# Where the transposes of the small convolution rows stand: among the keys' projections or in the dilated attention

## The chip, the core and the metric

One core of a Trainium2 chip runs the whole kernel in one launch. The metric is device time in microseconds of one execution; a kernel's time is the median over several executions. The engines spoken of here are TensorE (PE, with its weight loads, PEld), VectorE (DVE), ScalarE (ACT), GpSimd (POOL) and SyncE (SP), whose queue issues all DMA transfers of this kernel.

## The reference, cut to what matters

The kernel computes one layer of a decoder trunk on 256 positions and 1024 channels, in float32. A token mixer has three branches that read one input projection: block-sparse attention (8 heads), a short gated convolution, and dilated attention (12 heads in 3 groups). A gated feed-forward part with its own depthwise convolution follows, and each half ends in a residual and a layer norm.

```python
y_conv = b_gate * causal_dwconv(c_gate * hc, w_short_conv)      # 3 taps x 512 channels
y_dil = dilated_mixture(heads(qd, DIL_HEADS), heads(kd, DIL_HEADS), heads(vd, DIL_HEADS))
...
u = causal_dwconv(x @ w_up, w_ffn_conv) + b_ffn_conv            # 3 taps and a bias x 5632 channels
gate, val = jnp.split(u, 2, axis=-1)
return (jax.nn.silu(gate) * val) @ w_down
```

The change concerns the small operands `w_short_conv`, `w_ffn_conv` and `b_ffn_conv`. They lie in memory as rows along the channels; the convolutions want one number per channel, with the channels on the partitions.

## The kernel before, in words

**Matrix products.** Every float32 product is made of three matmuls (`mm3`, lines 229 to 231) on operands that are split into a high and a low part. A split is a cast on ACT (line 168) and a subtraction on DVE (line 169). The weights come through three `raw` buffers of 1 MB; each is split into four pieces of 128x512, up to ten pieces ahead of their use (`prep`, `LEAD`).

**The order of the work.** `project` makes two halves of 24 matmuls of 256 columns each into an `acc` buffer (three of them), and `by_tokens` makes steps of 12 matmuls of 512 columns. After each half or step stands a `tick`. It prepares the next weight pieces, consumes the result if one is complete, and takes one function off the list `side`. So `side` spreads the attention's work between the projections. A planner then puts the instructions of each engine in an order of its own: an instruction written later may be moved ahead into a place where the engine would stand idle by the planner's reckoning. The buffers of one pool are handed out in the order in which the code first writes them; in the program of before this holds for all 70 `att` buffers and all 759 `b` buffers without an exception.

**Around the change.** The stage runs: the dilated attention's queries (the third group by line 523), its keys (three groups, six halves and six ticks, lines 526 and 527), its values (`project_tokens` with four ticks, `project_tokens_half` with two), then the values of the block-sparse attention (`project_tokens` again, four ticks, line 534), then the short convolution's C and h (lines 552 and 553). `keys` consumes a half on ACT (lines 311 and 313) and DVE (lines 317 and 318); the last line-318 subtraction frees the `acc` buffer. `dilated` gives seven functions for each of two head pairs `p` and `q`: scores, second scores, normalisation, two turns by transposes (line 347), the product with the values, and the outputs. Scores are matmuls of line 326 into `att` buffers, of which there are five.

**The small rows.** `small_loads` issues five DMAs on SP's queue into `row1` and `row2`, which take 2 of the 61 `b` buffers. `small_weights` transposes them: one transpose of 12 rows (line 484) and four of 44 rows (line 486) on PE into one `att` buffer, then two copies on DVE, to `sconv` (line 487) and to `fconv` (line 488). `sconv` is first read by line 547 in the short convolution, `fconv` by `taps` (lines 700 and 702) in the feed-forward part.

Of the kernel before, what the change touches and what calls it, by code (L numbers as in the profile page):

```python
# [37 lines left out]
def trunk(ctx: ExitStack, tc, x, w_in, w_short_conv, w_moba_proj, w_dil_proj, w_conv_proj, w_mix_out,  # L38
# [133 lines left out]
    side, late = [], []  # L172
# [90 lines left out]
    def project_tokens():  # L263

        vs = [(buf(F32R, (P, 2, 256)), buf(F32R, (P, 2, 256))) for _ in range(2)]

        def consume(t, o):
            for i, (vh, vl) in enumerate(vs):
                split(o[:, 256 * i:256 * i + 256], vh[:, t, :], vl[:, t, :])

        by_tokens(of_x, KT, consume)
        return vs
# [16 lines left out]
    def queries(store):  # L289

        def consume(c, o):
            q = buf(F32R, (P, 2, T))
            for a in range(2):
                s = HALF[a]
                nc.scalar.copy(q[s, a, :], o[s, :])
            for a in range(2):
                s, n = HALF[a], HALF[1 - a]
                nc.vector.tensor_sub(q[n, a, :], o[s, :], q.bitcast(F32)[s, a, :])  # L298
            store.append(q)
        return consume  # L300
# [116 lines left out]
    def moba(c, q, k, v, y):  # L417
        es, en, ps = [], [], []

        def score():  # L420
            e1, e0 = etiles()
            es.extend((e1, e0))
            for a in range(2):
                o = att((P, 2, T))
                for t in range(2):
                    scores(o[:, t, :], q[c], k[c], a, t)
                e = e1[:, a * T:a * T + T], e0[:, a * P:a * P + P]
                en.append(exponentials(e[0], [(e[0], o[:, 1, :], maskm.rearrange("p a c -> p (a c)"))]))
                en.append(exponentials(e[1], [(e[1], o[:, 0, 0:P], maskm[:, 1, :])]))

        def normal():
            while en:
                normalized(*en.pop(0))

        def turn():
            e1, e0 = es
            p0 = turned([e0[:, 0:P], e1[:, 0:P], e0[:, P:2 * P], e1[:, 2 * P:3 * P]])
            h, l = turned([e1[:, P:2 * P], e1[:, 3 * P:4 * P]])
            ps.append((p0, (h[:, 0:2, :], l[:, 0:2, :])))

        def value():
            ps.append(values([v], ps, c))

        return [score, normal, turn, value, lambda: outputs(ps[1], y)]

    def both(*fs):
        return lambda: [f() for f in fs]
# [27 lines left out]
    def small_loads():  # L475
        nc.sync.dma_start(row1[0:12], w_short_conv.rearrange("j (t c) -> (j t) c", c=P))
        for j in range(3):
            nc.sync.dma_start(row2[0:2 * NJ, j, :], w_ffn_conv[j].rearrange("(t c) -> t c", c=P))
        nc.sync.dma_start(row2[0:2 * NJ, 3, :], b_ffn_conv[0].rearrange("(t c) -> t c", c=P))
# [37 lines left out]
    for g in range(2):  # L517
        q = queries(dq[g])
# [3 lines left out]
    for g in range(2, 3):  # L522
        project(queries(dq[g]), ahead=0)
    small_loads()
    side += [lambda: None] * 4 + [small_weights]
    for g in range(3):
        project(keys(dk[g]), ahead=0)
    assert not side
    yd = [buf(F32R, (P, 2, T)) for _ in range(2)]
    p, q = (dilated(c, dq, dk, dv, [t[:, c, :] for t in yd]) for c in range(2))  # L530
    side += [p[0], p[1], p[2], q[0], p[3], p[4], q[1], p[5], q[2], p[6], q[3], q[4], q[5], q[6]]
    dv.extend(project_tokens())
    dv.append(project_tokens_half())
    mv = project_tokens()
# [3 lines left out]
    for b in range(2):  # L538
# [21 lines left out]
        p, q = (moba(c, mq, mk, mv[b], [t[:, c, :] for t in ym]) for c in range(2))  # L560
# [244 lines left out]
```

## Time and profile before

| what | value |
|---|---|
| median of 3 runs | 476.15 us (474.7, 476.15, 476.85) |
| profiled execution | 475.9 us, of which the span from the first to the last instruction is 474.1 us |
| busy share of PE, DVE, ACT | 98%, 75%, 57% of the span |
| data moved | 83.45 MB, mean 176 GB/s |
| mean granted TensorE clock | 0.992 of full speed |

The profile is one execution. Times in its views are microseconds from the start of the span. A row of the timeline gives the start, the duration, the engine, the line, the operation, the tile written and the tiles read, and, in brackets, how long the engine stood idle before and what ended that. Matmuls are pipelined: each lasts longer than the distance from its start to the next one's, so costs on PE are read as distances between starts.

### The profile page before, as it was taken

The numbers are of one execution on the slowest core, as the hardware profiler recorded it, in microseconds if no ns is written. First come the engines' busy times: TensorE is split into PE (matmuls) and PEld (weight loads), VectorE is DVE, ScalarE is ACT, GpSimd is POOL, SyncE is SP. The second block draws the span as 40 slices with busy tenths as digits, with TensorE's granted clock in tenths as the row PEclk, the third lists the DMA queues.
The fourth block names the chain that finished last, engine by engine and source line by source line (L and its number), as shares of the span: only waits on it lengthen the run. The fifth ranks groups of instructions, "written<-read, shape, count | busy, mean of one in ns | idle before, by whom it ended". The sixth has DMA issues, their size and how long they took to land.

```text
span 474.1 us, 8155 instructions
## 1 busy us (share of the span) xinstructions
PE 463.7 (98%) x3095; PEld 426.3 (90%) x3095; DVE 355.5 (75%) x756; ACT 268.4 (57%) x568; POOL 10.4 (2%) x29
## 2 busy tenths in 40 slices
PE   8989999999999999999999999999999999999993
PEld 6989898999999888888888899999999999999983
DVE  5895998678989944775477966997767686786866
ACT  4894585736667844634463325876565565664710
POOL 1100000010100000000000000000000000000000
PEclk9998999999999999999999999999999999999998
DMA  8963665653544654646554804557455646637202
GB/s 283 325 205 105 197 183 176 224 178 90 178 130 138 187 201 168 220 159 207 191 211 146 266 1 154 201 179 267 157 199 178 198 157 205 225 107 248 105 1 88
DMA packets 57739, 83.45 MB, mean 176 GB/s; under 512 B 1705, under 2 KB 41317, under 8 KB 57701
## 3 DMA queue, kind: packets, MB, share of 16 engines
q1 hardware_dynamic: 57700, 82.94, 52.7%
q8 instruction: 24, 0.39, 0.4%
q14 instruction: 15, 0.11, 0.1%
HBM read 81.89 MB, written 1.05 MB: 175 GB/s over the span
## 4 chain that ended last, share of the span: by engine, by line
PE 94%; DMA 2%; DVE 2%; issue 1%; SPq 0%; ACT 0%; DVEq 0%
PE acc L229 23%; PE acc L231 22%; PE acc L230 22%; PE att L230 7%; PE att L229 7%; PE att L231 7%; PE att L326 2%; PE att L347 1%; DMA b<-in_w_ffn_conv_dram 1%; PE acc L499 1%; PE att L499 1%; DMA xs<-in_x_dram 1%; DVE b L169 1%; DVE b L298 0%; PE att L588 0%
## 5 line engine op out<-in xcount | busy, mean ns | idle before, releaser
L169 DVE TENSOR_TENSOR b<-raw,b 128x512 fp32r<-128x512 f32 x300 | 194.0, 686 | 41.6 <-ACT b L168 38.7
L168 ACT CAST b<-raw 128x512 fp32r<-128x512 f32 x288 | 160.2, 619 | 2.4 <-DMA raw<-in_w_up_dram 2.1
L229 PE MATMUL acc<-x1Th,b 128*128 128x256 f32 x320 | 90.9, 284 | 0.0
L231 PE MATMUL acc<-x1Th,b 128*128 128x256 f32 x320 | 90.6, 283 | 0.0
L230 PE MATMUL acc<-x1Tl,b 128*128 128x256 f32 x320 | 90.5, 283 | 0.0
L229 PE MATMUL acc<-xTh,b 128*128 128x256 f32 x224 | 64.8, 289 | 0.4 <-DVE b L298 0.4
L230 PE MATMUL acc<-xTl,b 128*128 128x256 f32 x224 | 63.9, 285 | 0.0
L231 PE MATMUL acc<-xTh,b 128*128 128x256 f32 x224 | 63.9, 285 | 0.0
L230 PEld LDWEIGHTS acc<-x1Tl,b 128*128 128x128 f32 x320 | 61.4, 192 | 0.1
L229 PEld LDWEIGHTS acc<-x1Th,b 128*128 128x128 f32 x320 | 61.4, 192 | 0.1
L231 PEld LDWEIGHTS acc<-x1Th,b 128*128 128x128 f32 x320 | 61.4, 192 | 0.0
L702 DVE SCALAR_TENSOR_TENSOR b<-acc,fconv,b 128x255 f32<-128x255 f32 x80 | 38.3, 479 | 30.3 <-ACT b L700 29.3
L229 PE MATMUL att<-b,b 128*128 128x512 f32 (+1 forms) x170 | 59.1, 348 | 0.0
L230 PE MATMUL att<-b,b 128*128 128x512 f32 (+1 forms) x170 | 58.9, 347 | 0.0
L231 PE MATMUL att<-b,b 128*128 128x512 f32 (+1 forms) x170 | 58.7, 346 | 0.0
L229 PE MATMUL acc<-b,xTh 128*128 128x512 f32 (+1 forms) x144 | 54.7, 381 | 0.0
L230 PE MATMUL acc<-b,xTh 128*128 128x512 f32 (+1 forms) x144 | 54.4, 378 | 0.0
L231 PE MATMUL acc<-b,xTl 128*128 128x512 f32 (+1 forms) x144 | 54.4, 378 | 0.0
L229 PEld LDWEIGHTS acc<-xTh,b 128*128 128x128 f32 x224 | 43.6, 194 | 0.8 <-PE acc L231 0.6
L230 PEld LDWEIGHTS acc<-xTl,b 128*128 128x128 f32 x224 | 43.6, 195 | 0.0
L231 PEld LDWEIGHTS acc<-xTh,b 128*128 128x128 f32 x224 | 43.5, 194 | 0.0
L700 ACT ACTIVATE b<-acc,fconv 128x256 f32<-128x256 f32 x40 | 22.6, 564 | 28.7 <-PE acc L231 28.6
(118 smaller groups left out, 649.2 us busy)
## 6 DMA issues: line engine op xcount, KB each, us to landing
raw<-in_w_in_dram SPq DMA_DIRECT2D x30, 1024.0 KB, 5.4
raw<-in_w_up_dram SPq DMA_DIRECT2D x22, 1024.0 KB, 5.2
raw<-in_w_down_dram SPq DMA_DIRECT2D x11, 1024.0 KB, 5.0
raw<-in_w_mix_out_dram SPq DMA_DIRECT2D x4, 1024.0 KB, 4.9
raw<-in_w_in_dram SPq DMA_DIRECT2D x12, 256.0 KB, 5.5
raw<-in_w_conv_proj_dram SPq DMA_DIRECT2D x4, 512.0 KB, 4.8
raw<-in_w_moba_proj_dram SPq DMA_DIRECT2D x4, 512.0 KB, 5.1
xs<-in_x_dram SPq DMA_DIRECT2D x4, 256.0 KB, 4.9
```

The costliest lines, as they stand in the source:

```text
L168: nc.scalar.copy(h, src)
L169: nc.vector.tensor_sub(l, src, h.bitcast(F32))
L229: nc.tensor.matmul(o, ah, bh, start=first, stop=False)
L230: nc.tensor.matmul(o, ah, bl, start=False, stop=False)
L231: nc.tensor.matmul(o, al, bh, start=False, stop=last)
L326: nc.tensor.matmul(o, qt, k[i][:, a, :], start=i == 0, stop=i == 1)
L347: nc.tensor.transpose(p[:, i, :], b, ident)
L499: last = nc.tensor.matmul(o[c], w[i][:, c * P:c * P + P], xt[:, k, :], start=k + part == 0, stop=k == KT - 1 and i == 1)
L700: nc.scalar.activation(v, o, AF.Identity, bias=w[3], scale=w[0])
L702: nc.vector.scalar_tensor_tensor(v[:, j:], o[:, :T - j], w[j], v[:, j:], op0=OP.mult, op1=OP.add)
```

## The change

`small_weights` is no longer the fifth function that the keys' ticks take (after the first half of the third group). It is taken together with `q[2]`, the normalisation of the second head pair, in the third tick of the block-sparse attention's value projection. The five DMAs of `small_loads` stay where they were, and the list `side` is as long as before in that stage; the keys' six ticks now take nothing. `both` calls its functions one after the other.

```diff
     small_loads()
-    side += [lambda: None] * 4 + [small_weights]
     for g in range(3):
         project(keys(dk[g]), ahead=0)
     assert not side
     yd = [buf(F32R, (P, 2, T)) for _ in range(2)]
     p, q = (dilated(c, dq, dk, dv, [t[:, c, :] for t in yd]) for c in range(2))
-    side += [p[0], p[1], p[2], q[0], p[3], p[4], q[1], p[5], q[2], p[6], q[3], q[4], q[5], q[6]]
+    side += [p[0], p[1], p[2], q[0], p[3], p[4], q[1], p[5], both(q[2], small_weights), p[6], q[3], q[4], q[5], q[6]]
     dv.extend(project_tokens())
```

## Prediction

> **What bounds the kernel now.** I read the page first: the busy shares, the clock row and the chain that ended last.
>
> ```profile
> span 474.1 us, 8155 instructions
> PE 463.7 (98%) x3095; PEld 426.3 (90%) x3095; DVE 355.5 (75%) x756; ACT 268.4 (57%) x568; POOL 10.4 (2%) x29
> PEclk9998999999999999999999999999999999999998
> PE 94%; DMA 2%; DVE 2%; issue 1%; SPq 0%; ACT 0%; DVEq 0%
> ```
>
> PE is busy 98% of the span and makes 94% of the chain, so a microsecond taken off PE's stream is a microsecond off the end, if nothing else comes late in its place. The clock row has one 8 inside the kernel, in the fourth slice of 11.85 us (36 to 47 us). Next come PE's waits over the whole span, and the chain in the stretch from 28 to 37 us.
>
> ```profile
> PE acc L193 <- DVE warm L188: 1.2, 1, 1.2
> PE att L486 <- DMA b<-in_w_ffn_conv_dram: 1.1, 2, 0.6
> PE acc L229 <- DVE b L298: 0.4, 1, 0.4
> ```
>
> ```profile
> 30.01 5.63 DMA b<-in_w_ffn_conv_dram
> ```
>
> Only three waits exist on PE. One is in the warm-up, the last waits for the consumption of a query (line 298), and the one between them belongs to the change: the transposes of line 486 wait for the feed-forward rows, whose DMA stands on the chain from 30.0 us on for 5.63 us. PE's timeline shows what happens there.
>
> ```profile
> 33.58 0.28 PE L231 MATMUL acc<-xTh,b 128*128 128x256 f32 x1
> 33.79 0.23 PE L484 MATMUL att<-ident,b 12*128 12x12 f32 x1
> 34.52 0.26 PE L486 MATMUL att<-ident,b 44*128 44x44 f32 x1 [0.50 <-DMA b<-in_w_ffn_conv_dram]
> 34.70 0.38 PE L326 MATMUL att<-b,b 128*128 128x256 f32 x1
> 35.69 0.26 PE L486 MATMUL att<-ident,b 44*128 44x44 f32 x1 [0.61 <-DMA b<-in_w_ffn_conv_dram]
> 35.88 0.44 PE L326 MATMUL att<-b,b 128*128 128x256 f32 x1
> 36.24 0.33 PE L486 MATMUL att<-ident,b 44*128 44x44 f32 x1
> 36.51 0.58 PE L229 MATMUL acc<-xTh,b 128*128 128x256 f32 x1
> ...
> 39.59 0.28 PE L231 MATMUL acc<-xTh,b 128*128 128x256 f32 x1
> 39.71 0.28 PE L229 MATMUL acc<-xTh,b 128*128 128x256 f32 x1
> ...
> 43.55 0.28 PE L231 MATMUL acc<-xTh,b 128*128 128x256 f32 x1
> 43.76 0.26 PE L486 MATMUL att<-ident,b 44*128 44x44 f32 x1
> 43.95 0.38 PE L229 MATMUL acc<-xTh,b 128*128 128x256 f32 x1
> ```
>
> The planner moved four of the five transposes ahead, between the two halves of the keys' second group, and two score matmuls with them. PE takes its queue in order. The half that starts at 36.51 had to stand behind transposes whose rows had not landed. The fifth transpose is at 43.76.
>
> **A second loss follows the gap.** The windows view gives busy time by engine, the granted clock and the DMA share.
>
> ```profile
> 36.20:39.60 3.40, 3.40 (x17) 3.28 (x17) 2.35 (x5) 0.00 (x0) 0.00 (x0) 0.52 0.76 264
> 39.60:43.00 3.40, 3.40 (x31) 3.40 (x30) 0.00 (x0) 1.99 (x5) 0.00 (x0) 1.00 0.00 0
> ```
>
> Right after the gap the granted clock is 0.52 for 3.4 us, and 17 matmuls pass where the next 3.4 us pass 31. DVE does nothing from 39.6 to 43.0 and the DMA share is 0: DVE's own queue is held too.
>
> ```profile
> 44.05 0.17 DVE L487 COPY sconv<-att 128x12 f32<-128x12 f32 x1 [5.43 <-PE att L486]
> ```
>
> **The change part by part: what goes.**
>
> 1. The gap. Matmuls of this form start 0.12 us apart (39.59 to 39.71), so the stream before the gap ends at 33.70 and the next half starts at 36.51: 2.81 us. The two score matmuls remain. They cost 0.12 us each, by the chain's row of twelve:
>
> ```profile
> 53.79 1.43 PE att L326 x12
> ```
>
> That leaves 2.81 - 0.24 = 2.57 us.
>
> 2. The half clock. From 36.51 to 39.59 there are 14 starts. At 0.12 us they would take 1.68 instead of 3.08 us: 1.40 us.
>
> [...] This gap is 2.81 us with seven small matmuls in it, and yet 0.52 stands behind it.
>
> 3. The fifth transpose at 43.76: 43.55 to 43.95 is 0.40 where 0.12 is usual, so 0.28 us.
>
> Together 2.57 + 1.40 + 0.28 = 4.25 us off PE's path.
>
> **What is late next.** The half at 36.51 would start near 33.95, the third group's halves near 36.83 and 39.71 (24 x 0.12 = 2.88 apart). Each needs the `acc` buffer of the half three before it, freed when DVE's two subtractions of line 318 are done:
>
> ```profile
> 31.75 0.88 DVE L318 TENSOR_TENSOR b<-acc,b 64x256 fp32r<-64x256 f32 x2
> 34.41 0.86 DVE L318 TENSOR_TENSOR b<-acc,b 64x256 fp32r<-64x256 f32 x2
> 37.04 0.86 DVE L318 TENSOR_TENSOR b<-acc,b 64x256 fp32r<-64x256 f32 x2
> ```
>
> That is 32.63, 35.27 and 37.90, with 1.3 us or more to spare each time; none of this DVE work waits for a transpose. After it DVE runs on at 38.62 instead of standing until 44.05, so it moves ahead by up to 5.43 us where PE moves by 4.25. The weights are there too:
>
> ```profile
> L169 DVE TENSOR_TENSOR b<-raw,b 128x512 fp32r<-128x512 f32 x27 | 17.5, 688 | 1.1 <-ACT b L160 0.8
> ```
>
> ```profile
> 46.92 0.40 PE L229 MATMUL acc<-b,xTh 128*128 128x512 f32 x1
> ```
>
> The first row groups DVE's subtractions up to 44.1 us: 27 pieces are split. The keys end with piece 24, and PE reaches piece 25, the first of the values, only at 46.92. The raw load that follows piece 28 stands behind DVE's stall today and comes earlier without it. The five DMAs on SP's queue keep their place. `row1` and `row2` hold 2 of 61 buffers some 40 us longer; that costs one piece of lead of up to ten, nothing while the lead holds.
>
> **What comes.** The same five transposes at the third tick of the value projection, one step before the C projection at 85.23:
>
> ```profile
> 85.23 0.28 PE L229 MATMUL acc<-xTh,b 128*128 128x256 f32 x1
> ```
>
> One step is some 3 us, so near 82 us, or 78 after the shift; the place need not be known closer. The rows landed over 40 us before, so nothing waits. No row of before shows five such transposes in a run. Bounds: twelve 128x128 transposes, row of line 347 below, take 66.07 - 64.84 = 1.23 us, 0.10 each, so 0.5 us; and the lone one of 0.28 five times, 1.40 us. Below nothing is excluded, since PE is full there. I take 0.28 for the first and 0.12 for each further one, 0.76 us, nearer to the row of twelve because they too stand together.
>
> ```profile
> 64.84 1.47 PE L347 MATMUL att<-ident,e 128*128 128x128 f32 x12
> 66.07 0.36 PE L229 MATMUL acc<-b,xTh 128*128 128x256 f32 x1
> ```
>
> [...] The twelve at 64.84 are followed by a granted clock of 1.00:
>
> ```profile
> 66.00:72.00 6.00, 6.00 (x43) 5.56 (x42) 5.89 (x15) 5.67 (x15) 0.00 (x0) 1.00 0.50 145
> 72.00:78.00 6.00, 6.00 (x35) 5.27 (x34) 6.00 (x18) 4.09 (x9) 0.00 (x0) 1.00 0.23 58
> 78.00:84.00 6.00, 6.00 (x31) 5.06 (x30) 2.96 (x7) 1.68 (x4) 0.00 (x0) 1.00 0.94 301
> ```
>
> DVE's two copies (0.17 us by its row, and the larger one of the same kind, bounded by a 128x512 subtraction at 0.69) I cost at nothing: DVE is busy 2.96 of 6.00 us there. A copy that waits for the transposes holds what is queued behind it, weight splits above all. If that cover were gone it would cost at most its own 0.9 us and the wait. The first reader comes much later:
>
> ```profile
> 96.47 0.35 DVE L547 TENSOR_SCALAR b<-b,sconv 128x256 f32<-128x256 f32 x1
> ```
>
> **The sum**, against the profiled execution: 475.9 - 4.25 + 0.76 = 472.4 us. The profile lies 0.25 us under the median of 476.15, and the runs shown span 474.7 to 476.85, so the forecast is 3.75 us or 0.8% under the median.
>
> **The rivals.**
>
> *The half clock stays.* If those 3.4 us came from something else than the gap, or fall on another thin place of PE in the new alignment, the 1.40 us are not gained: 473.8 us. [...] Against it: the half clock starts within 0.3 us of the gap's end and appears nowhere else inside the kernel.
>
> *DVE becomes the bound.* It is busy 5.89 and 6.00 of 6.00 us from 66 to 78. If its chain there could not start earlier, PE would run into it and gain only the lead it has over DVE now. No row shows that lead; I take one split of 0.69 us (the row of 27): 475.9 - 0.69 = 475.2 us. Against it: 5.43 us of DVE's idling go just before.
>
> *The change does not do what it says.* The planner could move the transposes ahead into the same gap: 475.9 us. Against it: `att` buffers are handed out in written order, and some 18 now stand ahead of this one, with five in the pool.
>
> *Slower.* DVE's copies could be planned ahead of the score reductions and weight splits around 72 to 78 us, where DVE has no free time, with their transposes far behind on PE. A wait like today's, 5.43 us, then holds the reductions; PE, which needs their results to go on, stands for the same time and pays 1.40 us of half clock again: 472.4 + 6.8 = 479.2 us. It decides once the copies wait longer than PE's lead over DVE, which was 1.3 to 1.8 us at the three line-318 rows. Against it: the copies can only follow transposes that themselves follow the first value product.
>
> **How the numbers follow.** Forecast 0.72, half clock stays 0.10, DVE bound 0.08, not moved 0.06, slower 0.04. A difference under 0.5% (2.4 us, bound 473.8) cannot be told from none. Faster: 0.72. Same: the next three, 0.24. Slower: 0.04. The range: the costs' bounds give 475.9 - 4.25 + 0.5 = 472.2 to 475.9 - 4.25 + 1.4 = 473.1; the spread of the runs about the profile, -1.2 and +0.95, makes it 471.0 to 474.0; with the half-clock rival (473.8 + 0.95) it reaches 474.7 and holds 0.82.
>
> **What would show it.** PE's timeline near 34 us: two score matmuls and then at once the half of 24, no wait on a row DMA. The clock row: no 8 in the fourth slice. DVE: no 5.4 us before `sconv`. PE near 78: five small transposes within 0.5 to 1.4 us, clock 1.00. Every later stage 3.5 us earlier. The prediction is wrong if PE shows new waits on `acc` or `att` buffers or on splits between 36 and 80 us, if the transposes stand anywhere ahead of the first value product, or if a half clock appears elsewhere.

## The result and the profile after

The changed kernel takes **472.85 us** (median of 4 runs, 472.68 to 472.98), the kernel before 476.1 us (4 runs, 474.7 to 476.85). The ratio is 0.9938 with a 95% interval of [0.9915, 0.9962]: faster by 0.4 to 0.85%. The profiled execution takes 472.95 us, its span is 471.2 us.

The page of the kernel after: its head, PE's share, the clock by slices and the chain that ended last.

```profile
span 471.2 us, 8149 instructions
PE 460.7 (98%) x3095; PEld 423.9 (90%) x3095; DVE 355.5 (75%) x756; ACT 268.2 (57%) x568; POOL 10.4 (2%) x29
PEclk9999999999999999999999999999999999999998
PE 95%; DVE 2%; DMA 1%; issue 0%; SPq 0%; ACT 0%; DVEq 0%
```

PE has as many instructions as before and 3.0 us less busy time. The 8 in the fourth slice is gone. PE's waits over the whole span after (who waited for whom, us in total, times, longest):

```profile
PE acc L193 <- DVE warm L188: 1.2, 1, 1.2
PE att L222 <- DMA xs<-in_x_dram: 0.8, 2, 0.4
PE acc L499 <- ACT b L160: 0.5, 1, 0.5
PE acc L229 <- DVE b L298: 0.4, 1, 0.4
```

The wait on `in_w_ffn_conv` is gone and none like it has come: from 36 us to the end no wait of PE is listed. Two short waits at the very start (lines 222 and 499, before 20 us) are new. PE's timeline after, at the old place:

```profile
34.23 0.28 PE L231 MATMUL acc<-xTh,b 128*128 128x256 f32 x1
34.35 0.40 PE L326 MATMUL att<-b,b 128*128 128x256 f32 x2
34.59 0.28 PE L229 MATMUL acc<-xTh,b 128*128 128x256 f32 x1
```

and at the new one:

```profile
78.59 0.39 PE L231 MATMUL acc<-b,xTl 128*128 128x512 f32 x1
78.91 0.23 PE L484 MATMUL att<-ident,b 12*128 12x12 f32 x1
79.07 0.44 PE L486 MATMUL att<-ident,b 44*128 44x44 f32 x4
79.44 0.50 PE L229 MATMUL acc<-b,xTh 128*128 128x512 f32 x1
```

At the old place the planner keeps the two score matmuls and the next half follows at once. At the new one the five transposes stand in a run and wait for nothing. The windows view after, with the stretches that were shown of before (columns: length, then busy time and count of PE, PEld, DVE, ACT and POOL, granted clock, DMA share, GB/s):

```profile
36.20:39.60 3.40, 3.40 (x30) 3.40 (x30) 3.33 (x7) 2.44 (x7) 0.00 (x0) 1.00 0.88 292
39.60:43.00 3.40, 3.40 (x31) 3.40 (x30) 3.25 (x8) 2.39 (x6) 0.00 (x0) 1.00 0.50 146
78.00:84.00 6.00, 6.00 (x37) 5.00 (x36) 1.94 (x7) 1.88 (x6) 0.00 (x0) 1.00 0.92 332
```

From 36.2 to 39.6 us PE passes 30 matmuls where it passed 17, at a clock of 1.00. DVE and the DMAs, which stood still from 39.6 to 43.0, now work through it. DVE's copies wait at the new place too, for less, and no wait of PE follows from it:

```profile
79.55 0.17 DVE L487 COPY sconv<-att 128x12 f32<-128x12 f32 x1 [2.36 <-PE att L486]
```

**Where the 2.95 us between the two profiled executions come from.** The two spans don't start alike. The input landed later in the execution after, 5.59 us from its issue where it was 4.91; the first row is of the kernel before, the second of the kernel after:

```profile
7.15 0.66 PE L222 MATMUL att<-ident,xs 128*128 128x128 f32 x4
```

```profile
7.83 0.66 PE L222 MATMUL att<-ident,xs 128*128 128x128 f32 x4 [0.36 <-DMA xs<-in_x_dram]
```

By the old place the kernel after is 34.23 - 33.58 = 0.65 us late, and it was so already at 19.28 us against 18.63, in front of everything that the change touches. So the stretches are compared by a mark inside the program: the start of the last matmul before the old place. From it to the end of the span the kernel before takes 474.12 - 33.58 = 440.54 us, the kernel after 471.17 - 34.23 = 436.94: **3.60 us**, which the change gives.

The same two marks for every profile below (starts in us on PE's timeline). "Third queries" is the third group of the dilated attention's queries, "next half" the half of the keys that follows the old place:

| kernel | third queries' first matmul | last matmul before the old place | next half's first | C projection's first | span | mark (column 3) to end |
|---|---|---|---|---|---|---|
| before | 18.63 | 33.58 | 36.51 | 85.23 | 474.12 | 440.54 |
| after | 19.28 | 34.23 | 34.59 | 82.30 | 471.17 | 436.94 |
| after, again | 18.77 | 33.94 | 34.30 | 82.00 | 471.06 | 437.12 |
| pinned | 18.26 | 33.21 | 33.33 | 81.23 | 470.16 | 436.95 |
| early rows | 18.88 | 33.99 | 34.11 | 81.30 | 470.21 | 436.22 |
| early rows, again | 18.66 | 33.66 | 33.78 | 80.96 | 469.76 | 436.10 |
| none | 20.35 | 35.29 | 35.65 | 82.60 | 471.60 | 436.31 |
| fill | 18.95 | 33.91 | 36.63 | 85.15 | 473.94 | 440.03 |
| long gap | 19.02 | 34.60 | 43.38 | 91.52 | 480.40 | 445.80 |
| long gap, filled | 18.32 | 33.38 | 41.05 | 88.31 | 477.16 | 443.78 |

### The profile page after: what moved, and what is told of

Its sections match the earlier page's. It is cut to its first block, busy times and chain, and to the rows that moved or that the text cites. A ratio compares the mean times of both kernels' runs of the same rounds, so it can differ in the third digit from the quotient of the medians.

```text
span 471.2 us, 8149 instructions
## 1 busy us (share of the span) xinstructions
PE 460.7 (98%) x3095; PEld 423.9 (90%) x3095; DVE 355.5 (75%) x756; ACT 268.2 (57%) x568; POOL 10.4 (2%) x29
## 4 chain that ended last, share of the span: by engine, by line
PE 95%; DVE 2%; DMA 1%; issue 0%; SPq 0%; ACT 0%; DVEq 0%
PE acc L229 23%; PE acc L231 23%; PE acc L230 23%; PE att L229 7%; PE att L230 7%; PE att L231 7%; PE att L326 2%; PE att L347 1%; DMA xs<-in_x_dram 1%; PE acc L499 1%; PE att L499 1%; DVE b L169 1%; DVE b L298 0%; PE att L587 0%; PE att L222 0%
## 5 line engine op out<-in xcount | busy, mean ns | idle before, releaser
L229 PE MATMUL acc<-xTh,b 128*128 128x256 f32 x224 | 63.8, 285 | 0.4 <-DVE b L298 0.4
L231 PE MATMUL acc<-xTh,b 128*128 128x256 f32 x224 | 63.4, 283 | 0.0
L229 PEld LDWEIGHTS acc<-xTh,b 128*128 128x128 f32 x224 | 42.9, 192 | 0.7 <-PE acc L231 0.6
L231 PEld LDWEIGHTS acc<-xTh,b 128*128 128x128 f32 x224 | 42.9, 192 | 0.0
```

The costliest lines, as they stand in the source:

```text
L229: nc.tensor.matmul(o, ah, bh, start=first, stop=False)
L231: nc.tensor.matmul(o, al, bh, start=False, stop=last)
```

## The experiments

The first four ran on one chip, beside 10 runs of the kernel before with a median of 474.79 us; the last four on another, beside 17 runs with a median of 475.7 us.

**Pinned.** The transposes stay where the kernel before has them in the code, but behind the last matmul written ahead of them (`behind` makes what a function writes follow a given instruction of the same engine).

```diff
+    newest = [None]
     def mm3(o, ah, al, bh, bl, first, last):
...
-        nc.tensor.matmul(o, al, bh, start=False, stop=last)
+        newest[0] = nc.tensor.matmul(o, al, bh, start=False, stop=last)
...
-    side += [lambda: None] * 4 + [small_weights]
+    side += [lambda: None] * 4 + [lambda: behind(newest[0], small_weights)]
```

> The transposes stay in the keys' ticks, but are pinned behind the last matmul of the third group's first half, so that the planner cannot move them into the earlier gap. Theory (PE's queue stood behind rows that had not landed, and the half clock followed): the rows have landed by 36 us, so no wait, granted clock 1.00 from 36 to 43 us, and the time is that of the changed kernel, 472.3 to 473.2 us or 0.7% under the kernel before. Rival (the place in the keys' projections is the cost, through the att buffer or DVE's two copies): little change, 475 us or more.

Measured: 472.59 us (6 runs), ratio 0.9958 [0.9944, 0.9972]; from the mark to the end 436.95 us, the changed kernel's 436.94. PE's timeline of this kernel:

```profile
38.97 0.28 PE L233 MATMUL acc<-xTh,b 128*128 128x256 f32 x1
39.18 0.23 PE L486 MATMUL att<-ident,b 12*128 12x12 f32 x1
39.34 0.44 PE L488 MATMUL att<-ident,b 44*128 44x44 f32 x4
39.71 0.38 PE L231 MATMUL acc<-xTh,b 128*128 128x256 f32 x1
```

The same five transposes among the keys' projections, 0.74 us from matmul to matmul, no wait. The place in the code was not the cost. The planner's moving four of them ahead of rows that had not landed was.

**Early rows.** Only the DMAs move.

```diff
     in_order.clear()
+    small_loads()
     for g in range(2):
         q = queries(dq[g])
...
-    small_loads()
     side += [lambda: None] * 4 + [small_weights]
```

> The kernel before, with the five row DMAs issued ahead of the queries' consumption instead of behind the third group's queries; the transposes keep their place in the list. Theory: the wait goes and the half clock with it; five transposes together cost some 0.7 us, part of it inside the 0.4 us that PE waits near 27 us anyway: 472.0 to 472.8 us, clock 1.00 from 36 to 43 us. Rival (the place is the cost): 475 us or more. Second rival (earlier DMAs delay the weights): new waits on splits or raw buffers before 30 us, 473.5 us or more.

Measured: 471.91 us (4 runs), ratio 0.9946 [0.9928, 0.9965]. PE has no wait on the rows, and none on a split.

> The kernel with the early row DMAs once more, beside the changed kernel on one chip. Theory: its five transposes stand in PE's wait near 27 us (0.4 us) and cost 0.2 to 0.3 us instead of 0.65, so it is 0.3 to 0.5 us under the changed kernel. Rival (the order of the rest decides): no difference, or the changed kernel is faster.

Measured in the second batch: 473.17 us (7 runs), against 472.84 us (11 runs) of the changed kernel beside it. The medians do not settle it, because the runs of each kernel fall into two groups. Of the early rows' 11 runs in both batches, six lie at 471.4 to 472.0 and five at 473.2 to 473.6. Of the changed kernel's 15, twelve lie at 472.3 to 473.0 and three at 474.4 to 474.6. Group by group the early rows are 1 us under the changed kernel, and the second batch had four of seven runs in their upper group. PE's timeline in the second batch's profile:

```profile
27.18 0.28 PE L231 MATMUL acc<-xTh,b 128*128 128x256 f32 x1
27.39 0.23 PE L484 MATMUL att<-ident,b 12*128 12x12 f32 x1
27.55 0.44 PE L486 MATMUL att<-ident,b 44*128 44x44 f32 x4
27.92 0.38 PE L229 MATMUL acc<-xTh,b 128*128 128x256 f32 x1
```

The same place in the changed kernel, where PE waits for a query's consumption:

```profile
27.80 0.28 PE L231 MATMUL acc<-xTh,b 128*128 128x256 f32 x1
28.52 0.36 PE L229 MATMUL acc<-xTh,b 128*128 128x256 f32 x1 [0.44 <-DVE b L298]
```

The distance is 0.74 us with the transposes and 0.72 without them: they stand in a wait that is there anyway and cost next to nothing. In the other profile of each kernel the distances are 0.89 with them and 0.95 without. Since they stand ahead of the mark here, the kernels are compared from the third queries' first matmul to the end: this kernel takes 451.1 and 451.3 us, the changed kernel 451.9 and 452.3. It is the better version by the traces, by 0.6 to 1.2 us; by medians alone that is open.

**None.** What the transposes cost at their new place. The edit is against the changed kernel; it leaves out the five transposes and two copies, and with zeros for their constants the results of both convolutions.

```diff
+    nc.gpsimd.memset(sconv, 0.0)
+    nc.gpsimd.memset(fconv, 0.0)
...
-    side += [p[0], p[1], p[2], q[0], p[3], p[4], q[1], p[5], both(q[2], small_weights), p[6], q[3], q[4], q[5], q[6]]
+    side += [p[0], p[1], p[2], q[0], p[3], p[4], q[1], p[5], q[2], p[6], q[3], q[4], q[5], q[6]]
```

> The changed kernel without the five transposes and the two copies: the convolutions' constants are zeros set on GpSimd, so both convolutions and what follows from them are left out of the result, while every other instruction stays. Theory: the transposes at their new place cost PE the 0.6 to 0.8 us that its timeline shows, so 472.0 to 472.3 us against 472.85. Rival (they are hidden there): 472.8 us.

Measured: 471.67 us (4 runs), somewhat under the 472.0 to 472.3 expected. Its profiled execution is the slowest of the four, 473.4 us. In it the third queries start at 20.35 us instead of 18.3 to 19.3, and behind that nothing is late; so a late start may be what makes the upper groups, but this is one execution. From the mark to the end it takes 436.31 us, 0.63 and 0.81 us less than the changed kernel's two profiles. So the transposes are not hidden at the new place; they cost what PE's timeline shows.

**Fill.** PE works through the wait of the kernel before.

```diff
+        idle = att()
         for j in range(4):
+            for _ in range(4 if j < 3 else 0):
+                nc.tensor.matmul(idle, warm[:, :P], warm, start=True, stop=True)
             nc.tensor.transpose(p[:, 64 + n * j:64 + n * j + n], row2[0:n, j, :], ident[0:n, 0:n])
```

> The kernel before, with four warm-up matmuls of 512 bf16 columns, 0.22 us each, in front of each of the first three transposes of 44 rows; the planner puts nine of the twelve into the gap and three to the fifth transpose. The wait on the rows stays, but PE is busy in it. Theory (the gap's idling throttles the clock): granted clock 1.00 from 36 to 40 us, the half after the gap back at 0.12 us a matmul, so 1.4 us won and some 0.5 us paid for the extra matmuls outside the wait: 475.0 us, 0.2% under the kernel before. Rival (the half clock has another cause): clock still 0.5 there, 476.4 us or more.

Measured: 475.98 us (5 runs), ratio 1.0039 [1.0014, 1.0064]: slower, where 0.2% faster was expected. The windows view of this kernel:

```profile
34.00:37.40 3.40, 3.24 (x18) 1.81 (x18) 3.28 (x8) 2.14 (x5) 0.00 (x0) 1.00 0.59 168
37.40:40.80 3.40, 3.40 (x31) 3.40 (x30) 2.05 (x4) 0.90 (x3) 0.00 (x0) 1.00 0.58 177
```

The clock is 1.00, as the theory wants, but that decides nothing here: none of the 10 runs of the kernel before on this chip shows the half clock either. Their mean clocks are 0.995 to 0.997, where the profiled execution of before had 0.992. The mean can tell this, though it varies for another reason too: the profiles of before and after have some half clock at their end, when PE is done. That is about 4.5 us before (0.78 from 469 to 470 us, 0.50 from there on) and 2.5 us after (0.83 from 468.4 to 468.8 us, 0.50 from there on; mean 0.997). The changed kernel's other profile has a mean of 0.994, an estimated 5.7 us at half speed (twice 0.006 of its 471.1 us). By the same estimate another 3.4 us at half speed are 0.36% of the span and would bring either to 0.994 or less. So the extra matmuls were paid and nothing was saved; from the mark to the end they cost an estimated 0.9 us (440.03 against the 440.54 of before less 1.40 for its half clock). The half clock is not in every execution, which the next runs take up.

**The changed kernel again**, with more runs of the kernel before beside it.

> The changed kernel itself, beside the kernel before on the same chip and in the same session as the three below. In the runs of the kernel before that stand beside the second batch of experiments the mean granted clock was 0.995 to 0.997 and not 0.992: the half clock after the gap is then not in every execution, and the median gain is the gap and the fifth transpose less the new place. Theory: 2.57 + 0.28 - 0.65 = 2.2 us, 0.46%, where the kernel before shows 0.995 or more; rival (the half clock is always there): 3.4 us, 0.72%.

Measured: 472.84 us (11 runs), ratio 0.9946 [0.9928, 0.9963], so 0.54%, nearer to the theory's 0.46% than to 0.72%, though the interval holds both. The clocks decide. Of the 17 runs of the kernel before, 5 have a mean clock of 0.990 to 0.993 and lie at 475.7 to 477.9 us, median 476.24; the other 12 have 0.995 or more and a median of 475.14. None of the changed kernel's 15 runs is under 0.994. Against 472.84 the twelve give 2.30 us, where the theory has 2.2; the five give 3.40 us, where the rival has 3.4. The half clock is thus in some executions of the kernel before and not in others, and the gain over each kind is near what its sum says, though the runs of a kind spread over 2 to 3 us.

**Long gap, and long gap filled.** The rows come later, the transposes are pinned into the gap, and in the second kernel PE has other work there.

```diff
+    def gap():
+        behind(loading[0], small_loads)
+        held_by.append(small_weights(newest[0]))
-    small_loads()
-    side += [lambda: None] * 4 + [small_weights]
+    side += [lambda: None] * 2 + [gap] + [lambda: None] * 2
...
+        for _ in range(32):
+            last = behind(last, nc.tensor.matmul, idle, warm[:, :P], warm, True, True)
```

The last two lines stand in the filled kernel alone. In both, each transpose is queued behind the one before it, and the next half's first matmul behind the last transpose.

> The kernel before, with the row DMAs issued behind the raw load at 34 us and the five transposes pinned between the second group's halves, so that PE stands for some 7 us instead of 2.8. Theory (a long idle stretch of PE throttles its clock): PE waits on the rows until some 41 us, the granted clock is 0.5 for some 3.4 us behind that in the profile, mean 0.992 or less in every run, and the time is 4.5 us of gap and 1.4 us of clock over the kernel before's undisturbed 474.8: 480.0 to 481.5 us. Rival (the half clock is by chance, whatever PE does): mean clock 0.995 or more in most runs, 479 us.

Measured: 482.01 us (4 runs, 481.3 to 483.1), above the 480.0 to 481.5 expected; mean clock 0.989 in all four. PE's wait and the windows of this kernel:

```profile
PE att L160 <- DMA b<-in_w_short_conv_dram: 6.1, 1, 6.1
```

```profile
34.70:40.90 6.20, 0.18 (x2) 0.00 (x0) 5.39 (x11) 2.14 (x5) 0.00 (x0) 0.90 0.62 188
40.90:46.50 5.60, 5.52 (x23) 4.87 (x24) 1.03 (x4) 0.00 (x0) 0.00 (x0) 0.50 0.59 187
46.50:52.00 5.50, 5.50 (x48) 5.50 (x47) 2.60 (x6) 3.31 (x9) 0.00 (x0) 1.00 0.00 0
```

> The same, with 32 warm-up matmuls of 512 bf16 columns, 0.22 us each, ahead of the transposes, so that PE works through the same wait for some 7 us. Theory: granted clock 1.00 from 34 to 46 us and 0.995 or more in every run, and the time is that of longgap less the 1.4 us: 478.5 to 480 us. Rival (the half clock is by chance): no difference between the two in the clock.

Measured: 479.43 us (4 runs), mean clock 0.995 in all four. Its windows:

```profile
33.50:40.30 6.80, 6.80 (x34) 3.05 (x32) 5.30 (x11) 2.14 (x5) 0.00 (x0) 1.00 0.61 177
40.30:46.50 6.20, 6.20 (x52) 5.91 (x51) 1.51 (x5) 2.14 (x5) 0.00 (x0) 1.00 0.47 165
```

The same place, once idle and once filled: by the mean clocks half clock in four of four runs (0.989), then in none of four (0.995). With PE idle there the half clock came (0.50 from 40.9 to 46.5 us), with PE at work it did not (1.00). It also lasted longer than expected: 0.90 over 6.2 us is 1.2 us at half, and with the 5.6 us behind it that makes 6.8 us instead of 3.4. The filled kernel is 2.6 us faster by the medians and 2.0 from the mark to the end, where 1.4 was expected. The longer half clock explains more than 1.4, but the sum is not exact: from the last matmul to the first transpose the filled kernel takes 7.14 us (33.38 to 40.52; its 32 extra matmuls are busy for 7.08 of them, 0.22 each) and the idle one 6.38 (34.60 to 40.98).

## Why the prediction was right, step by step

- **The gap (predicted 2.57 us): right.** From the last matmul to the next half it was 36.51 - 33.58 = 2.93 us and is 34.59 - 34.23 = 0.36: 2.57 us.
- **The half clock (predicted 1.40 us): the mechanism right, its weight in the median too large.** In the profiled execution it is all there: the stretch from that half's start to the third group's last half shrinks from 43.95 - 36.51 = 7.44 us to 40.35 - 34.59 = 5.76, which is 1.68, the 1.40 of the clock and the 0.28 of the fifth transpose. But only 5 of the 27 runs of the kernel before beside the experiments show a low clock. That explains why the median moved by 2.9 us in the second comparison where 3.75 was forecast; for the first one's 3.25 us the clocks of the runs before are not on record. The prediction took the one profiled execution for the median one, and that its forecast of over 0.5% held was in part luck: beside the first experiments, where no run before shows the half clock, the pinned kernel, which equals the changed one from the mark on, was only 0.42% under the kernel before (0.28% to 0.56%). The rival "the half clock stays" named the wrong cause: an idle PE did bring it in the long gap (mean clock 0.989 in four of four runs, 0.995 with the gap filled), only not at every gap of 2.8 us (5 of 27).
- **Two readings that are off.** The gap holds six small matmuls (four transposes, two of scores) and not seven, and the half clock begins some 0.4 us before the gap's end and not within 0.3 us of it (0.69 is granted from 36.00 to 36.20 us already). Neither enters the sum.
- **The fifth transpose (0.28 us): right**, within the 1.68 us above.
- **The new place (predicted 0.76 us): 0.62 us.** 79.44 - 78.59 is 0.85 us where 0.23 us is usual. The kernel without the transposes is 0.63 us shorter from the mark on than this profile. The bounds of 0.5 and 1.40 us held. In their run here they overlap: the four of 44 rows are busy for 0.44 us together, where the lone one of before was for 0.26, and 0.62 us for five is 0.12 each.
- **Nothing late next: right.** PE has no wait on an `acc` or `att` buffer or on a split from 36 us on, so DVE, which runs on where it stood 5.43 us, is not the bound.
- **The copies at nothing: right**, though they wait 2.36 us for the transposes. DVE is busy 1.94 of 6.00 us there.
- **The rivals.** DVE as the bound and the planner's moving the transposes back are refuted by the timeline. The slower case did not come: the copies' wait of 2.36 us is followed by no wait of PE.
- **The sum.** 2.57 + 1.68 - 0.62 = 3.63 us against 3.60 from the mark to the end. The start, 0.65 us later in the execution after, makes it 2.95 between the two profiles. The forecast of faster by over 0.5% holds for both medians (0.62% and 0.54%), but both intervals reach below it (0.38% and 0.37%).

## What to carry to other kernels

An instruction that a planner moves into a gap is only free if its inputs are there on the chip by then (here they were not, and PE's path was 2.57 us longer): when PE waits on a small DMA, look whether the waiting instruction stands ahead of work that was ready. Load small operands early, or pin their use behind the work that is ready; either gave here what moving the use 45 us later gave, and early rows, with the transposes in a wait that existed anyway, gave 0.6 to 1.2 us more by the traces. Compare two profiles from a mark behind the start, since the start alone can differ by 2 us (third queries at 18.26 to 20.35 us here).

## What the runs showed of the hardware that was not expected

A gap of 2.8 us on PE with six small matmuls in it, and no listed wait over 0.61 us, came with a half clock in the profiled execution (0.52 over 3.4 us) and, by the mean clocks, in 5 of 27 runs (0.990 to 0.993 against 0.995 or more); one of 6.1 us without any work came with it in four of four (mean 0.989), and for longer (the 5.6 us of work after it stood at 0.50). With 32 bf16 matmuls in the long gap it stayed away in four of four (mean 0.995, and 1.00 from 33.5 to 46.5 us in the profile). What decides which executions pay for the short gap is not shown.

The start of this kernel differs by up to 2 us between the profiles here (third queries at 18.26 to 20.35 us), by 0.5 us between the two of the changed kernel (18.77 and 19.28), and a later start is in the span. What decides it was not tried.
